# Coarser squares, sums and roots, and pairwise adds in the last five loads, in a power-average pooling kernel (p = 2)

## The chip, the cores and the metric

The kernel runs on one core of one Trainium2 chip. The metric is the device time of one execution in microseconds (us), as the median of several.

## The reference

```python
x = np.random.randn(32, 256, 4096).astype(np.float32)      # p = 2.0, kernel_size = 4
for i in range(out_length):                                # 1024 windows of 4 neighbours
    window = np.abs(x[:, :, 4*i:4*i+4]) ** p
    result[:, :, i] = np.mean(window, axis=-1) ** (1.0 / p)
```

So each output is the root of a quarter of the sum of four squares. 134.2 MB are read and 33.6 MB written.

## The kernel before

The input is taken as 128 rows of columns. 22 loads (18 of 13,184 columns, then three of 6,592 and one of 5,056) go through three input slots (on-chip buffers that are used in turn). Two loads (at the end three, then one) make a group, which has one store. Each load is cut in pieces. A piece is squared in place on ScalarE, summed by fours on VectorE with a reduce, and rooted on ScalarE one piece later.

```python
W, O_W = 13184, 6592
X_SLOTS, O_SLOTS = 3, 2
slots = [[(W, [4416, 4384, 4384])]] * 18          # one slot: (columns of a load, its pieces)
slots += [[(6592, [3296, 3296])] * 2, [(6592, [3296, 3296]), (5056, [2528, 2528])]]
groups = [2] * 9 + [3, 1]                         # loads in each store
late = {7, 8, 9, 10}                              # stores issued from the load queue, after all loads
in_x = {9, 10}                                    # groups whose outputs go into an input slot
# ... (load(), store() and the list of loads cut) ...
def root(g, o, ends):
    nc.scalar.activation(out=o, in_=o, func=Act.Sqrt, scale=1.0 / k)
    if ends and g not in late:
        store(g, nc.scalar)
# ... main loop, over loads i: loads up to two slots ahead are issued first (cut)
    for step in chunks:
        v = xs[i][:, c:c + step]
        nc.scalar.activation(out=v, in_=v, func=Act.Square)
        o = ots[g][:, at + c // k:at + (c + step) // k]
        nc.vector.tensor_reduce(out=o, in_=v.rearrange("p (n j) -> p n j", j=k),
                                axis=mybir.AxisListType.X, op=mybir.AluOpType.add)
        if pending is not None:
            root(*pending)
        c += step
        pending = (g, o, i == firsts[g] + groups[g] - 1 and c == w)
root(*pending)
for g in sorted(late):
    store(g, nc.sync)
```

Of the kernel before, what the change touches and what calls it, by code (L numbers as in the profile page):

```python
# [1 line left out]

# [4 lines left out]


@with_exitstack
def kernel(  # L10
    ctx: ExitStack,
    tc: tile.TileContext,
    x: bass.AP,
    p: float,
    kernel_size: int,
    out: bass.AP,
):






    nc = tc.nc

    assert float(p) == 2.0, "kernel specialized for p == 2"
    k = int(kernel_size)
    assert k == 4, "kernel specialized for kernel_size == 4"

    P = nc.NUM_PARTITIONS  # L30
    fp32 = mybir.dt.float32
    Act = mybir.ActivationFunctionType
    xf = x.rearrange("b c l -> (b c l)")
    of = out.rearrange("b c l -> (b c l)")
    total = xf.shape[0] // P

    W, O_W = 13184, 6592
    X_SLOTS, O_SLOTS = 3, 2
    slots = [[(W, [4416, 4384, 4384])]] * 18
    slots += [[(6592, [3296, 3296])] * 2, [(6592, [3296, 3296]), (5056, [2528, 2528])]]  # L40
    groups = [2] * 9 + [3, 1]
    late = {7, 8, 9, 10}
    in_x = {9, 10}


    loads = [(s, sum(w for w, _ in slot[:j]), *slot[j]) for s, slot in enumerate(slots)
             for j in range(len(slot))]
    n = len(loads)
    assert sum(w for _, _, w, _ in loads) == total

    firsts = [sum(groups[:g]) for g in range(len(groups))]
    assert sum(groups) == n
    group_of = [g for g, count in enumerate(groups) for _ in range(count)]
    columns = [sum(w for _, _, w, _ in loads[firsts[g]:firsts[g] + groups[g]])
               for g in range(len(groups))]

    x_pool = ctx.enter_context(tc.tile_pool(name="x_pool", bufs=X_SLOTS))
    o_pool = ctx.enter_context(tc.tile_pool(name="o_pool", bufs=O_SLOTS))
    ctx.enter_context(tc.manual_schedule())

    def block(flat, g, div):
        at, width = sum(columns[:g]) * P // div, columns[g] * P // div
        return flat[at:at + width].rearrange("(p w) -> p w", p=P)

    slot_tiles = {}
    xs = {}

    def load(i):
        s, at, w, _ = loads[i]
        if at == 0:  # L70
            slot_tiles[s] = x_pool.tile([P, W], fp32, name="xt")
        v = slot_tiles[s][:, at:at + w]
        g = group_of[i]
        src = sum(loads[j][2] for j in range(firsts[g], i))
        nc.sync.dma_start(out=v, in_=block(xf, g, 1)[:, src:src + w])  # L75
        xs[i] = v

    ots = {}

    def store(g, queue):  # L80
        queue.dma_start(out=block(of, g, k), in_=ots[g])  # L81

    def root(g, o, ends):
        nc.scalar.activation(out=o, in_=o, func=Act.Sqrt, scale=1.0 / k)  # L84
        if ends and g not in late:
            store(g, nc.scalar)

    ahead = 0
    while ahead < n and loads[ahead][0] < X_SLOTS - 1:
        load(ahead)  # L90
        ahead += 1
    pending = None
    for i in range(n):
        s, _, w, chunks = loads[i]
        while ahead < n and loads[ahead][0] < s + X_SLOTS:
            load(ahead)
            ahead += 1
        g = group_of[i]
        if i == firsts[g]:
            pool, width = (o_pool, O_W) if g not in in_x else (x_pool, W)  # L100
            t = pool.tile([P, width], fp32, name="ot" if g not in in_x else "xt")
            ots[g] = t[:, 0:columns[g] // k]
        at = sum(loads[j][2] for j in range(firsts[g], i)) // k
        assert sum(chunks) == w
        c = 0
        for step in chunks:
            v = xs[i][:, c:c + step]
            nc.scalar.activation(out=v, in_=v, func=Act.Square)  # L108
            o = ots[g][:, at + c // k:at + (c + step) // k]
            nc.vector.tensor_reduce(  # L110
                out=o, in_=v.rearrange("p (n j) -> p n j", j=k),
                axis=mybir.AxisListType.X, op=mybir.AluOpType.add,
            )
            if pending is not None:
                root(*pending)
            c += step
            pending = (g, o, i == firsts[g] + groups[g] - 1 and c == w)
    root(*pending)
    for g in sorted(late):
        store(g, nc.sync)  # L120


# [1 line left out]
_INS = ['x', 'p', 'kernel_size']  # L124
_OUTS = [((32, 256, 1024), 'float32')]

_NUMBERS = {'p': 2.0, 'kernel_size': 4}


# [26 lines left out]
```

## Time and profile before

| | before |
|---|---|
| time, median (3 runs) | 394.79 us (394.69 to 394.88) |
| span of the profile | 393.0 us |
| DMA packet time, both queues | 99.3% of the span |
| VectorE, ScalarE busy | 72%, 74% |

From the page of before, its busy times (engine, us, share, instructions) and its DMA share in 40 slices (tenths):

```profile
DVE 282.4 (72%) x62; ACT 292.4 (74%) x126; POOL 0.2 (0%) x4
...
DMA  8999999999999999999999999999999999999997
...
q1 hardware_dynamic: 3744, 144.15, 85.3%
q10 hardware_dynamic: 1008, 23.63, 14.0%
```

The last two lines are the load queue (with the late stores) and the store queue: packets, MB, share of the time of 16 DMA engines. Together they fill the span. Neither compute engine does. So the kernel is held by the DMA.

The groups of before by shape give the price of each instruction (count, then busy us in total and mean ns of one, then idle time before it):

```profile
L110 DVE TENSOR_REDUCE ot<-xt 128x1096 f32<-128x4384 f32 x36 | 169.9, 4719 | 6.7 <-ACT xt L108 6.4
L108 ACT ACTIVATE xt<-xt 128x4384 f32<-128x4384 f32 x36 | 138.3, 3843 | 2.9 <-ACT ot L84 2.9
L84 ACT ACTIVATE ot<-ot 128x1096 f32<-128x1096 f32 x36 | 39.7, 1103 | 1.1 <-DVE ot L110 0.9
```

With the other shapes this is 1.04 ns a column for the reduce and 0.84 ns for square and root, plus 0.15 to 0.18 us an instruction.

The timeline of before near the end (start us, us, engine, line, operation):

```profile
380.48 0.89 ACT L84 ACTIVATE xt<-xt 128x824 f32<-128x824 f32 x1 [0.67 <-DVE xt L110]
381.27 2.29 ACT L108 ACTIVATE xt<-xt 128x2528 f32<-128x2528 f32 x1
381.39 6.11 SPq L81 DMA_DIRECT2D out_dram<-xt  x2
...
386.42 0.73 ACT L84 ACTIVATE xt<-xt 128x632 f32<-128x632 f32 x1 [2.23 <-DVE xt L110]
```

The 0.89 us root finishes group 9, and its store is issued at 381.4. The last root ends at 387.15, and the last store follows. The DMA in stretches of that time (stretch, us, VectorE busy, ScalarE busy, POOL, clock, DMA share, GB/s) shows that it never waited for these stores:

```profile
380.00:385.00 5.00, 4.54 (x3) 3.71 (x3) 0.00 (x0) 1.00 0.95 407
385.00:390.00 5.00, 1.38 (x1) 0.73 (x1) 0.00 (x0) 1.00 0.96 411
390.00:393.00 3.00, 0.00 (x0) 0.00 (x0) 0.00 (x0) 1.00 0.35 143
```

From the page, the issue of the last two stores (size, us from issue to landing):

```profile
out_dram<-xt SPq DMA_DIRECT2D x1, 2472.0 KB, 9.3
out_dram<-xt SPq DMA_DIRECT2D x1, 632.0 KB, 5.0
```

### The profile page before, as it was taken

The page shows a single profiled execution, that of the slowest core. Times are in us where ns is not written, and L with a number is a line of the kernel's source. Part 1 is how long each engine was busy: PE and PEld are TensorE (multiplying, and loading weights), DVE is VectorE, ACT ScalarE, POOL GpSimd, SP SyncE. Part 2 cuts the span into 40 slices and gives each one's busy share as a digit, 9 for nine tenths or more (in the row PEclk, how much of TensorE's full clock was granted, in tenths as well). Part 3 has the DMA queues.
Part 4 walks back from the last instruction along what each step waited for, and adds up shares of the span by engine and source line. Part 5 has one row for each costly group of instructions (what it writes and reads, how often), then busy time and mean ns, then how long its engine had stood idle before and what let it go on. Part 6 is the DMA issues. An engine that isn't in the chain of part 4 may idle for free.

```text
span 393.0 us, 316 instructions
## 1 busy us (share of the span) xinstructions
DVE 282.4 (72%) x62; ACT 292.4 (74%) x126; POOL 0.2 (0%) x4
## 2 busy tenths in 40 slices
DVE  0068989494959495949594959595859686899992
ACT  1099986777786768686958695959595949899991
POOL 0000000000000000000000000000000000000000
DMA  8999999999999999999999999999999999999997
GB/s 344 429 429 440 429 424 381 443 459 429 413 440 435 429 427 432 429 440 441 437 448 421 432 462 435 392 429 472 429 413 451 425 429 429 424 429 427 438 429 329
DMA packets 4754, 167.79 MB, mean 427 GB/s; under 512 B 528, under 2 KB 528, under 8 KB 656
## 3 DMA queue, kind: packets, MB, share of 16 engines
q1 hardware_dynamic: 3744, 144.15, 85.3%
q10 hardware_dynamic: 1008, 23.63, 14.0%
q14 instruction: 2, 0.02, 0.0%
HBM read 134.22 MB, written 33.55 MB: 427 GB/s over the span
## 4 chain that ended last, share of the span: by engine, by line
DMA 62%; ACT 19%; DVE 14%; issue 2%; ACTq 0%; SPq 0%
DMA xt<-in_x_dram 62%; ACT xt L108 15%; DVE ot L110 11%; DVE xt L110 3%; ACT ot L84 3%; ACT xt L84 1%; ACTq L81 0%; SPq L75 0%; ACTq L108 0%
## 5 line engine op out<-in xcount | busy, mean ns | idle before, releaser
L110 DVE TENSOR_REDUCE ot<-xt 128x1096 f32<-128x4384 f32 (+1 forms) x54 | 255.4, 4731 | 102.7 <-ACT xt L108 102.4
L108 ACT ACTIVATE xt<-xt 128x4384 f32<-128x4384 f32 (+3 forms) x62 | 230.3, 3716 | 89.2 <-DMA xt<-in_x_dram 86.3
L84 ACT ACTIVATE ot<-ot 128x1096 f32<-128x1096 f32 (+1 forms) x54 | 59.8, 1108 | 1.8 <-DVE ot L110 0.9
L110 DVE TENSOR_REDUCE xt<-xt 128x824 f32<-128x3296 f32 (+1 forms) x8 | 27.0, 3384 | 1.3 <-ACT xt L108 1.2
L84 ACT ACTIVATE xt<-xt 128x824 f32<-128x824 f32 (+1 forms) x8 | 6.7, 841 | 3.0 <-DVE xt L110 2.9
L108 ACT ACT_TABLE_LOAD x1 | 1.3, 1283 | 0.7 <-PEq L137 0.7
L84 ACT ACT_TABLE_LOAD x1 | 1.3, 1283 | 0.0
L137 POOL MEMSET const-bfloat16-1.0<- 128x1 bf16 x1 | 0.1, 101 | 0.0
L137 POOL MEMSET const-uint8-127<- 128x1 uint8 x1 | 0.1, 101 | 0.0
L137 POOL MEMSET const-float32-0.0<- 128x1 f32 x1 | 0.1, 98 | 0.2 <-issue 0.2
L137 POOL MEMSET const-float32-1.0<- 128x1 f32 x1 | 0.1, 98 | 0.0
## 6 DMA issues: line engine op xcount, KB each, us to landing
xt<-in_x_dram SPq DMA_DIRECT2D x18, 6592.0 KB, 39.7
out_dram<-ot ACTq DMA_DIRECT2D x7, 3296.0 KB, 26.4
xt<-in_x_dram SPq DMA_DIRECT2D x3, 3296.0 KB, 24.6
out_dram<-ot SPq DMA_DIRECT2D x2, 3296.0 KB, 29.6
xt<-in_x_dram SPq DMA_DIRECT2D x1, 2528.0 KB, 26.4
out_dram<-xt SPq DMA_DIRECT2D x1, 2472.0 KB, 9.3
out_dram<-xt SPq DMA_DIRECT2D x1, 632.0 KB, 5.0
```

The costliest lines, as they stand in the source:

```text
L84: nc.scalar.activation(out=o, in_=o, func=Act.Sqrt, scale=1.0 / k)
L108: nc.scalar.activation(out=v, in_=v, func=Act.Square)
L110: nc.vector.tensor_reduce(out=o, in_=v.rearrange("p (n j) -> p n j", j=k), axis=mybir.AxisListType.X, op=mybir.AluOpType.add,)
L137: nc = _bacc.Bacc("TRN2", target_bir_lowering=False, num_devices=1)
```

## The change

The intent: fewer and larger instructions in the steady part (one square, one sum a load, one root a store), and a cheaper sum at the end. There two pairwise adds take the place of the reduce: they make half and then a quarter as many results as there are columns, 3/4 in all, where the reduce of before took 1.04 ns for every column. Tiles are now allocated once. The transfers stay as they were.

```diff
-    slots = [[(W, [4416, 4384, 4384])]] * 18
-    slots += [[(6592, [3296, 3296])] * 2, [(6592, [3296, 3296]), (5056, [2528, 2528])]]
+    slots = [[(W, [W])]] * 16 + [[(W, [6592, 6592])]] * 2
+    slots += [[(6592, [6592]), (6592, [6592])], [(6592, [6592]), (5056, [2528, 2528])]]
...
-    in_x = {9, 10}
+    in_x = {9: (2, 0), 10: (2, 4944)}
+    FINE, ENDS, LAG = {21}, {19, 20}, 1      # FINE: a root per piece; ENDS: a root per load
+    PAIRS = 17                               # pairwise adds from this load on
...
+    x_tiles = [x_pool.tile([P, W], fp32, name=f"xt{j}") for j in range(X_SLOTS)]
+    o_tiles = [o_pool.tile([P, O_W], fp32, name=f"ot{j}") for j in range(O_SLOTS)]
...
+    def total_sum(o, v, i):
+        if i < PAIRS:
+            nc.vector.tensor_reduce(...)     # as before
+            return
+        h = v.rearrange("p (m t) -> p m t", t=2)
+        nc.vector.tensor_tensor(out=h[:, :, 0], in0=h[:, :, 0], in1=h[:, :, 1], op=add)
+        q = v.rearrange("p (n j) -> p n j", j=k)
+        nc.vector.tensor_tensor(out=o, in0=q[:, :, 0], in1=q[:, :, 2], op=add)
...
-            if pending is not None:
-                root(*pending)
+            total_sum(ots[g][:, summed:summed + step // k], v, i)
+            while pending and pending[0][0] <= done - LAG:
+                root(*pending.pop(0)[1:])
+            done += 1
...
-            pending = (g, o, i == firsts[g] + groups[g] - 1 and c == w)
+            ends = summed == columns[g] // k
+            if ends or i in FINE or (i in ENDS and c == w):
+                pending.append((done - 1, g, ots[g][:, rooted:summed], ends))
+                rooted = summed
```

More of the change, by code (lines that the diff above doesn't have):

```diff
@@ L55 @@
                for g in range(len(groups))]
-    x_pool = ctx.enter_context(tc.tile_pool(name="x_pool", bufs=X_SLOTS))
-    o_pool = ctx.enter_context(tc.tile_pool(name="o_pool", bufs=O_SLOTS))
+    x_pool = ctx.enter_context(tc.tile_pool(name="x_pool", bufs=1))
+    o_pool = ctx.enter_context(tc.tile_pool(name="o_pool", bufs=1))
+    x_tiles = [x_pool.tile([P, W], fp32, name=f"xt{j}") for j in range(X_SLOTS)]
+    o_tiles = [o_pool.tile([P, O_W], fp32, name=f"ot{j}") for j in range(O_SLOTS)]
     ctx.enter_context(tc.manual_schedule())
@@ L63, in block @@
         return flat[at:at + width].rearrange("(p w) -> p w", p=P)
-    slot_tiles = {}
     xs = {}
@@ L69, in load @@
         s, at, w, _ = loads[i]
-        if at == 0:
-            slot_tiles[s] = x_pool.tile([P, W], fp32, name="xt")
-        v = slot_tiles[s][:, at:at + w]
+        v = x_tiles[s % X_SLOTS][:, at:at + w]
         g = group_of[i]
@@ L86, in root @@
             store(g, nc.scalar)
+    def total_sum(o, v, i):
+        add = mybir.AluOpType.add
+        if i < PAIRS:
+            nc.vector.tensor_reduce(
+                out=o, in_=v.rearrange("p (n j) -> p n j", j=k),
+                axis=mybir.AxisListType.X, op=add,
+            )
+            return
[3 more added lines that the diff above has]
+        nc.vector.tensor_tensor(out=o, in0=q[:, :, 0], in1=q[:, :, 2], op=add)
     ahead = 0
@@ L91 @@
         ahead += 1
-    pending = None
+    pending = []
+    done = 0
     for i in range(n):
@@ L99 @@
         if i == firsts[g]:
-            pool, width = (o_pool, O_W) if g not in in_x else (x_pool, W)
-            t = pool.tile([P, width], fp32, name="ot" if g not in in_x else "xt")
-            ots[g] = t[:, 0:columns[g] // k]
-        at = sum(loads[j][2] for j in range(firsts[g], i)) // k
+            t, first = (o_tiles[g % O_SLOTS], 0) if g not in in_x else (x_tiles[in_x[g][0]], in_x[g][1])
+            ots[g] = t[:, first:first + columns[g] // k]
+            summed = rooted = 0
         assert sum(chunks) == w
@@ L108 @@
             nc.scalar.activation(out=v, in_=v, func=Act.Square)
-            o = ots[g][:, at + c // k:at + (c + step) // k]
-            nc.vector.tensor_reduce(
-                out=o, in_=v.rearrange("p (n j) -> p n j", j=k),
-                axis=mybir.AxisListType.X, op=mybir.AluOpType.add,
-            )
-            if pending is not None:
-                root(*pending)
-            c += step
-            pending = (g, o, i == firsts[g] + groups[g] - 1 and c == w)
-    root(*pending)
+            total_sum(ots[g][:, summed:summed + step // k], v, i)
+            while pending and pending[0][0] <= done - LAG:
+                root(*pending.pop(0)[1:])
+            done += 1
+            c += step
+            summed += step // k
+            ends = summed == columns[g] // k
+            if ends or i in FINE or (i in ENDS and c == w):
+                pending.append((done - 1, g, ots[g][:, rooted:summed], ends))
+                rooted = summed
+    for job in pending:
+        root(*job[1:])
     for g in sorted(late):
```

## The prediction

> **What bounds the kernel now.** The DMA engines. The page's queue table gives them 85.3% + 14.0% = 99.3% of the 393.0 us span: 390.3 us of packet time, against 282 us (72%) for VectorE and 292 us (74%) for ScalarE. In the trace's packet records the first data packet starts 1.6 us into the span, the last ends near 391.6, with no hole between. At the usual packet times (1.947 us per 52,736 B, 0.978 us per 26,368 B) the traffic needs 387.7 us; 2.1 us are slower packets, at the start and at 40 to 70 us. So some 2 us are left to win, whatever the compute does.
>
> Compute touches the end. From the landing of load 17 (339.7 us) the timeline and the windows show ScalarE and VectorE both 90 to 100% busy until the last root (387.1): each small piece goes square, sum, root in turn. Two held-back stores (groups 7, 8) fill the DMA meanwhile. Group 9's store is issued at 381.4, while the queue is still busy, the last one (632 KB) at 387.2; it lands 5.0 us later.
>
> **What the change removes, adds, moves.** The DMA transfers keep count, sizes and layout. From the groups by shape, square and root cost 0.176 us + 0.836 ns a column, the reduce 0.153 us + 1.041 ns a column.
> - One 13,184-column square takes 11.2 us, its sum 13.9, a 6,592-column root 5.7. Some 65 small instructions go, at 0.15 to 0.18 us each: about 10 us of engine time, off the critical path.
> - A slot comes free 25 us after its load lands instead of about 18. Two later loads queue behind it (31 us of transfer at least), so the queue stays fed. Stores go out some 12 us later, which saves no traffic. Worth: 0.
> - Tail. My estimate, stepping both programs through these durations and a 434 GB/s queue, ends them together if a pairwise add runs at one column per 1.04 ns (10.6 us for a 13,184-column load instead of 13.9). With coarse pieces and reduce kept, the tail would be 5 us longer; the adds pay that back.
>
> **The disputed size** is the strided add: operands step two elements in the first add, four in the second. [...] No strided operand is in before's trace. [...] I think full rate likeliest (55%), a slow second add next (30%), both slow 15%.
>
> **Prediction.** 395.4 us, 8 in 10 between 394.0 and 400.5. Faster by over 2%: 1%; within 2%: 87%; slower by over 2%: 12%.
>
> **What would show each step.**
> - DMA share near 99%, packet time near 390 us: the bound holds. No hole between loads 2 and 3 (about 51 us): the feed holds.
> - 16 reduces near 13.9 us, squares near 11.2.
> - First add (6,592 outputs) 7.0 us, second (3,296) 3.6: full rate. [...]
> - The last root ends at 386 to 388 us.
>
> **What would make it wrong.** Slow strided adds [...]; coarse slots letting the DMA run dry early; a store held up by an output tile still being read; packets that become faster under fewer, longer instructions (up to 2 us won).

The forecast came to 395.4 us, 0.6 above before, with 394.0 to 400.5 as its range. Terms of it are cut where marked: two statements on the rate of strided operands, and the sizes given to slow adds (in ns a column and in us, and the time by which a slowed second add was to be known), since no trace of before shows them. "Full rate" is the 1.04 ns a column of before's reduce, carried over to an add that before does not have. The 434 GB/s agrees with the usual packet times: 16 times 52,736 B in 1.947 us is 433 GB/s.

## The result, and the profile after

| | before | after |
|---|---|---|
| time, median (6 runs each) | 394.80 us | 398.08 us (397.87 to 398.33) |
| ratio to before, 95% interval | | 1.0082 (1.0069 to 1.0095) |
| VectorE, ScalarE busy | 282.4, 292.4 us | 275.0, 281.7 us |
| last root ends | 387.15 us | 392.30 us |
| last DMA data packet ends | 391.7 us | 395.0 us |

The change costs 3.3 us, 0.8%, clearly outside the noise and within 2%.

The page of after:

```profile
DVE 275.0 (69%) x32; ACT 281.7 (71%) x40; POOL 0.2 (0%) x4
...
DMA  8999999999999999999999999999999999999967
...
q1 hardware_dynamic: 3744, 144.15, 84.5%
q10 hardware_dynamic: 1008, 23.63, 13.8%
```

Both compute engines do less work. The DMA moves the same packets in 98.3% of a longer span, 389.5 us against 390.3. What is new is the 6 in the last but one slice. The groups of after by shape:

```profile
L93 DVE TENSOR_REDUCE ot<-xt 128x3296 f32<-128x13184 f32 x16 | 222.2, 13886 | 105.1 <-ACT xt L123 105.1
L86 ACT ACTIVATE ot<-ot 128x6592 f32<-128x6592 f32 x9 | 51.2, 5683 | 2.9 <-DVE ot L101 2.9
L99 DVE TENSOR_TENSOR xt<-xt 128x3296 f32<-128x3296 f32 x5 | 17.9, 3587 | 4.6 <-ACT xt L123 4.6
L101 DVE TENSOR_TENSOR xt<-xt 128x1648 f32<-128x1648 f32 x3 | 9.5, 3155 | 0.1
L101 DVE TENSOR_TENSOR ot<-xt 128x1648 f32<-128x1648 f32 x2 | 6.2, 3119 | 0.1
```

Read the last three together. The first add (steps of two elements) makes 3,296 results in 3.59 us, 1.04 ns each after the fixed 0.15 us. The second (steps of four) makes half as many in nearly the same time, 3.155 us: 1.82 ns each. A piece of 6,592 columns costs 6.7 us this way, where the reduce costs 7.02.

The timeline of after, in the tail:

```profile
357.06 3.07 DVE L101 TENSOR_TENSOR ot<-xt 128x1648 f32<-128x1648 f32 x1
...
360.16 5.70 ACT L86 ACTIVATE ot<-ot 128x6592 f32<-128x6592 f32 x1 [2.91 <-DVE ot L101]
...
365.77 11.27 ACT L123 ACTIVATE xt<-xt 128x6592 f32<-128x6592 f32 x2
371.48 3.59 DVE L99 TENSOR_TENSOR xt<-xt 128x3296 f32<-128x3296 f32 x1 [4.62 <-ACT xt L123]
...
384.95 1.58 ACT L86 ACTIVATE xt<-xt 128x1648 f32<-128x1648 f32 x1 [1.45 <-DVE xt L101]
386.43 2.29 ACT L123 ACTIVATE xt<-xt 128x2528 f32<-128x2528 f32 x1
386.55 6.11 SPq L83 DMA_DIRECT2D out_dram<-xt  x2
...
391.57 0.73 ACT L86 ACTIVATE xt<-xt 128x632 f32<-128x632 f32 x1 [2.23 <-DVE xt L101]
```

ScalarE waits 2.91 us for the slow second add. Then it spends 5.70 us in one lumped root, and only then makes the next square. VectorE waits 4.62 us for that. Group 9's root ends 5.2 us later than in before, its store is issued at 386.55, and meanwhile the queue runs dry:

```profile
380.00:385.00 5.00, 4.97 (x3) 3.55 (x3) 0.00 (x0) 1.00 0.58 248
385.00:390.00 5.00, 3.86 (x3) 4.35 (x3) 0.00 (x0) 1.00 0.60 253
390.00:393.00 3.00, 1.50 (x2) 0.73 (x1) 0.00 (x0) 1.00 0.99 422
```

From the page of after, the last store's landing:

```profile
out_dram<-xt SPq DMA_DIRECT2D x1, 632.0 KB, 3.1
```

So the last root is 5.15 us later, the end only 3.3: the last store now lands 3.1 us after its issue instead of 5.0. The emptier queue is the likely reason; it was not tested by itself.

### The profile page after: what moved, and what is told of

Its sections match the earlier page's. It is cut to its first block, busy times and chain, and to the rows that moved or that the text cites. A ratio compares the mean times of both kernels' runs of the same rounds, so it can differ in the third digit from the quotient of the medians.

```text
span 396.2 us, 192 instructions
## 1 busy us (share of the span) xinstructions
DVE 275.0 (69%) x32; ACT 281.7 (71%) x40; POOL 0.2 (0%) x4
## 4 chain that ended last, share of the span: by engine, by line
DMA 47%; ACT 24%; DVE 22%; issue 6%; SPq 0%; ACTq 0%
DMA xt<-in_x_dram 47%; ACT xt L123 18%; DVE ot L93 14%; ACT ot L86 6%; DVE xt L99 4%; DVE xt L101 2%; DVE ot L101 2%; ACT xt L86 1%; ACT L86 0%; SPq L77 0%; ACTq L83 0%
## 5 line engine op out<-in xcount | busy, mean ns | idle before, releaser
L93 DVE TENSOR_REDUCE ot<-xt 128x3296 f32<-128x13184 f32 (+1 forms) x18 | 236.2, 13123 | 110.6 <-ACT xt L123 108.9
L123 ACT ACTIVATE xt<-xt 128x13184 f32<-128x13184 f32 (+2 forms) x25 | 223.1, 8937 | 102.0 <-DMA xt<-in_x_dram 100.2
L86 ACT ACTIVATE ot<-ot 128x6592 f32<-128x6592 f32 x9 | 51.2, 5683 | 2.9 <-DVE ot L101 2.9
L99 DVE TENSOR_TENSOR xt<-xt 128x3296 f32<-128x3296 f32 (+1 forms) x7 | 20.9, 2986 | 5.7 <-ACT xt L123 5.7
L101 DVE TENSOR_TENSOR xt<-xt 128x1648 f32<-128x1648 f32 (+1 forms) x5 | 12.1, 2411 | 0.2
L86 ACT ACTIVATE xt<-xt 128x632 f32<-128x632 f32 (+2 forms) x4 | 6.0, 1492 | 5.0 <-DVE xt L101 5.0
L101 DVE TENSOR_TENSOR ot<-xt 128x1648 f32<-128x1648 f32 x2 | 6.2, 3119 | 0.1
```

Source lines behind the costliest of these rows:

```text
L99: nc.vector.tensor_tensor(out=h[:, :, 0], in0=h[:, :, 0], in1=h[:, :, 1], op=add)
L101: nc.vector.tensor_tensor(out=o, in0=q[:, :, 0], in1=q[:, :, 2], op=add)
```

## The experiments

The theory after this reading: the second add's four-element step makes the loss, through the last root and the hole in the DMA. Rivals: (1) the lumped roots and large pieces in the tail make it; (2) the coarse part ahead of the tail (loads 0 to 15, "the front") or the fixed tiles do. All edits are against after, except where said. Twelve kernels ran: eleven correct, one (strides) wrong and run once.

| run | front, loads 0 to 15 | sums at the end | time, us | its before | ratio (95%) |
|---|---|---|---|---|---|
| compact | coarse | compact adds | 395.88 | 394.67 | 1.0030 (1.0017 to 1.0042) |
| reduce_tail | coarse | reduce | 398.97 | 394.67 | 1.0106 (1.0090 to 1.0121) |
| fine_roots | coarse | slow adds, root per piece | 396.03 | 394.67 | 1.0037 (1.0024 to 1.0049) |
| old_tail | coarse | as in before | 396.26 | 394.67 | 1.0041 (1.0029 to 1.0054) |
| old_front | as in before | slow adds | 396.86 | 394.74 | 1.0052 (1.0039 to 1.0065) |
| old_front_compact | as in before | compact adds | 394.85 | 394.74 | 0.9999 (0.9986 to 1.0011) |
| before_compact | before itself | compact adds | 395.16 | 394.74 | 1.0004 (0.9990 to 1.0018) |
| front_lump | fine, lumped root | compact adds | 394.61 | 394.64 | 0.9999 (0.9985 to 1.0012) |
| front_rootper | coarse, root per load | compact adds | 396.44 | 394.64 | 1.0040 (1.0026 to 1.0053) |
| compact_all | coarse | compact adds in all loads | 395.39 | 394.64 | 1.0017 (1.0004 to 1.0029) |
| front_late | fine, late lumped root | compact adds | 395.53 | 394.96 | 1.0013 (0.9999 to 1.0026) |

### compact: the same two adds without the four-element step

```diff
-        nc.vector.tensor_tensor(out=h[:, :, 0], in0=h[:, :, 0], in1=h[:, :, 1], op=add)
-        q = v.rearrange("p (n j) -> p n j", j=k)
-        nc.vector.tensor_tensor(out=o, in0=q[:, :, 0], in1=q[:, :, 2], op=add)
+        half = v[:, 0:v.shape[1] // 2]
+        nc.vector.tensor_tensor(out=half, in0=h[:, :, 0], in1=h[:, :, 1], op=add)
+        q = half.rearrange("p (n j) -> p n j", j=2)
+        nc.vector.tensor_tensor(out=o, in0=q[:, :, 0], in1=q[:, :, 1], op=add)
```

Expected: 

> Edit: the first pairwise add writes its results next to each other (front half of the same piece), so the second add steps two elements instead of four; all else as after. Theory (the second add's four-element step costs 1.82 ns a column instead of 1.04, 7.4 us more VectorE time in the last five loads, and this delays the last root): second add on 1,648 outputs 1.9 us instead of 3.16, last root ends near 387, no hole in the DMA at 380 to 390 us, time 394.6 to 395.3. Rival 1 (coarse roots and squares in the tail cost the time, not the adds): at least 397. Rival 2 (the coarse front and the fixed tiles cost it): 398.

Measured: 395.88 us (395.57 to 396.14). From the timeline of compact, one second add, the issue of the last two stores, and the last root:

```profile
378.58 1.87 DVE L102 TENSOR_TENSOR xt<-xt 128x1648 f32<-128x1648 f32 x1
...
382.09 5.65 SPq L83 DMA_DIRECT2D out_dram<-xt  x2
...
386.66 0.73 ACT L86 ACTIVATE xt<-xt 128x632 f32<-128x632 f32 x1 [1.77 <-DVE xt L102]
```

One stretch of its DMA, and from its page the last store's landing:

```profile
380.00:385.00 5.00, 3.36 (x4) 4.51 (x4) 0.00 (x0) 1.00 0.98 418
...
out_dram<-xt SPq DMA_DIRECT2D x1, 632.0 KB, 5.9
```

The second add fell from 3.155 to 1.87 us, the last root ends at 387.39 instead of 392.30, and the hole is gone. The loss against before falls from 3.3 to 1.2 us. Taking the four-element step away is thus enough to get back 2.1 us, but the time missed the expectation by 0.6 us: something else costs 1.2 us.

### reduce_tail: no pairwise adds

```diff
-    PAIRS = 17
+    PAIRS = 99
```

Expected: 

> Edit: reduce in all loads, no pairwise adds; all else as after. Theory: the pairwise add of a 6,592-column piece takes 6.75 us even with the slow second add, the reduce 7.02, so this is a little slower than after: 398.5 to 399.5. Rival (the pairwise adds as such are the mistake, the rest of the change is free): 394.8 to 395.3.

Measured: 398.97 us (398.37 to 399.27), 4.3 us over before and about 1 us over after. Even slow, the pairwise adds are no mistake against the reduce; they gain little of what they could.

### fine_roots: a root per piece in the tail, slow adds kept

```diff
-    FINE, ENDS, LAG = {21}, {19, 20}, 1
+    FINE, ENDS, LAG = set(range(16, 22)), {19, 20}, 1
```

Expected: 

> Edit: a root for every piece of loads 16 to 21 instead of one lumped root of 6,592 columns; slow adds kept; all else as after. Theory of the slow add alone: 397.5 to 398.3, as after. Rival 1 (the lumped root holds up the next squares by 5.7 us and starves VectorE, 4.6 us idle at 371 us): 395 or less. If both count, in between: my stepping of the instruction durations says 2.3 us less than after, 395.8.

Measured: 396.03 us (395.71 to 396.88), 1.4 us over before: 1.9 us better than after, with the slow adds untouched. From its timeline, one of the short roots, a second add that is as slow as ever, and the last root:

```profile
368.19 1.57 ACT L86 ACTIVATE xt<-xt 128x1648 f32<-128x1648 f32 x1
...
371.94 3.20 DVE L101 TENSOR_TENSOR xt<-xt 128x1648 f32<-128x1648 f32 x1
...
388.74 0.73 ACT L86 ACTIVATE xt<-xt 128x632 f32<-128x632 f32 x1 [2.24 <-DVE xt L101]
```

The last root ends at 389.47 instead of 392.30. So neither the slow add alone nor the lumped root alone is the cause: the expectation for both together, 395.8, is the one that came near. The chain at the end goes square, sum, root, next square, so a shorter root helps it as a shorter add does. Compact and fine_roots each get back about 2 of the 3.3 us. Whether the two repairs together, behind the coarse front, would gain more than either was not run.

### old_tail: the new front with before's tail

```diff
-    slots = [[(W, [W])]] * 16 + [[(W, [6592, 6592])]] * 2
-    slots += [[(6592, [6592]), (6592, [6592])], [(6592, [6592]), (5056, [2528, 2528])]]
+    slots = [[(W, [W])]] * 16 + [[(W, [4416, 4384, 4384])]] * 2
+    slots += [[(6592, [3296, 3296])] * 2, [(6592, [3296, 3296]), (5056, [2528, 2528])]]
-    FINE, ENDS, LAG = {21}, {19, 20}, 1
-    PAIRS = 17
+    FINE, ENDS, LAG = set(range(16, 22)), {19, 20}, 1
+    PAIRS = 99
```

Expected: 

> Edit: loads 0 to 15 as after (one square, one reduce, one root per store), loads 16 to 21 cut, summed and rooted as in before; fixed tiles kept. If the whole loss is made in the tail's own instructions: 394.8, as before. Rival 2 (the coarse front costs too, since load 15's single square, reduce and lumped root end some 4 us later and the tail starts late): 396 to 397.

Measured: 396.26 us (396.14 to 396.59), 1.6 us over before with the same tail instructions. So the front is not free. The last root of old_tail, from its timeline:

```profile
389.47 0.73 ACT L86 ACTIVATE xt<-xt 128x632 f32<-128x632 f32 x1 [2.23 <-DVE xt L93]
```

It ends 3.05 us later than before's, because the tail starts later: load 15's single square and reduce, and the 5.7 us lumped root of its group, stand in the way of load 16 (its second square starts at 333.17, in before at 328.90).

### old_front and old_front_compact: before's front with the new tail

```diff
-    slots = [[(W, [W])]] * 16 + [[(W, [6592, 6592])]] * 2
+    slots = [[(W, [4416, 4384, 4384])]] * 16 + [[(W, [6592, 6592])]] * 2
-    FINE, ENDS, LAG = {21}, {19, 20}, 1
+    FINE, ENDS, LAG = set(range(16)) | {21}, {19, 20}, 1
```

old_front_compact has the edit of compact besides.

Expected of old_front: 

> Edit: loads 0 to 15 as in before, in three pieces each; tail as in after with the slow second add. Theory (slow add and coarse front both count): between before and after, 396.2 to 397.2. Rival, tail alone: 398.1. Rival, front alone: 394.8.

Expected of old_front_compact: 

> Edit: the compact first add as in the run compact, and loads 0 to 15 cut, summed and rooted in three pieces as in before. The run compact ended 1.2 us above before with no common hole in the DMA: its 16 DMA engines ended up to 2.5 us apart, in before 1.0 us. Theory (the coarse front, with its later stores, leaves one DMA engine behind the others): landings 1 us apart, time 394.4 to 394.9. Rival (the new tail or the fixed tiles make the spread): 395.6 to 396.1, as compact.

Measured: old_front 396.86 us (396.61 to 397.21), old_front_compact 394.85 us (394.69 to 394.87). With the earlier runs this fills a table of two by two, as us over the before of the same rounds:

| | slow second add | compact adds |
|---|---|---|
| coarse front | +3.3 (after) | +1.2 (compact) |
| before's front | +2.1 (old_front) | +0.1 (old_front_compact) |

Before's front makes up only part of the loss when the slow adds stay: in old_front the last root still ends late, as its timeline shows.

```profile
390.61 0.73 ACT L86 ACTIVATE xt<-xt 128x632 f32<-128x632 f32 x1 [2.23 <-DVE xt L101]
```

The slow add, with the lumped roots kept, costs 2.0 to 2.1 us in either row and the coarse front 1.1 to 1.2 in either column. That the columns agree is partly chance, since the front works in two ways. With slow adds the last root sets the end, and the coarse front makes it 0.96 us later (392.30 against 391.34). With compact adds the last root is early enough in both, and the DMA engines set the end (below). The fixed tiles are in all four and cost nothing that shows, since old_front_compact is level with before. One number missed: old_front_compact's landings were 1.6 us apart at the end, not 1.

### before_compact: compact adds in the kernel before

```diff
-            nc.vector.tensor_reduce(...)
+            if i < 17:
+                nc.vector.tensor_reduce(...)      # as before
+            else:
+                ...                               # the two adds of the run compact
```

Expected: 

> Edit to the kernel before: in the last five loads the reduce is replaced by two pairwise adds, compact form; all else as before. Theory (before is held by the DMA to its last byte, and the compact adds are faster but off that path): last root 1 to 5 us earlier, time 394.4 to 394.9. Rival (the tail's compute holds before too): 393.5 or less.

Measured: 395.16 us (394.77 to 395.23), level with before within the interval; the median is 0.3 us above the expected range, which was too narrow. The last root ended at 385.05, 2.1 us earlier than in before, and gained nothing. Before is held by the DMA to its last byte.

### strides: the disputed add by itself

One load, then fp32 adds of 1,648 results at different steps, three of each, and squares. The result is wrong (most of the output is never written); the 140.45 us of this run mean nothing.

```python
def s(t, step, off):
    return t[:, 0:N * step].rearrange("p (n j) -> p n j", j=step)[:, :, off]
# L56 contiguous; L58, L60, L62, L66: both sources at step 2, 3, 4, 8; L64: step 4, neighbours;
# L68 one source at step 4; L70, L72 result at step 2, 4; L74 all three at step 4;
# L76 runs of two neighbours, hop of four. L48, L50, L52: squares, source at step 1, 2, 4; L54: result at 4
```

Expected: 

> Wrong result on purpose: one load, then fp32 adds of 1,648 outputs, three of each kind, with different steps of sources and result, and squares with steps. Theory[...]: step 1 and 2 of the sources 1.87 us, step 4 3.16 us, step 8 no faster than step 4, step 3 between; runs of two adjacent elements with a hop of four 1.87 us; a result step of 2 free, of 4 slow. Rival ([...]any step above one is slow[...]): step 2 near 3 us. Third: only two stepped sources together are slow: one source of step 4 at 1.87 us. No expectation for the squares but that step 2 is free.

Measured, from the groups of strides:

```profile
L66 DVE TENSOR_TENSOR dst<-src 128x1648 f32<-128x1648 f32 x3 | 9.3, 3113 | 0.1
...
L68 DVE TENSOR_TENSOR dst<-src 128x1648 f32<-128x1648 f32 x3 | 9.2, 3082 | 0.1
...
L62 DVE TENSOR_TENSOR dst<-src 128x1648 f32<-128x1648 f32 x3 | 9.2, 3062 | 0.1
...
L60 DVE TENSOR_TENSOR dst<-src 128x1648 f32<-128x1648 f32 x3 | 7.0, 2333 | 0.1
...
L56 DVE TENSOR_TENSOR dst<-src 128x1648 f32<-128x1648 f32 x3 | 5.6, 1875 | 48.3 <-ACT dst L54 48.2
L58 DVE TENSOR_TENSOR dst<-src 128x1648 f32<-128x1648 f32 x3 | 5.6, 1874 | 0.1
L76 DVE TENSOR_TENSOR dst<-src 128x1648 f32<-128x1648 f32 x3 | 5.6, 1874 | 0.1
```

Contiguous operands took 1.875 us (L56) and sources at step 2 took 1.874 (L58), so step 2 is free here, and so are runs of two with a hop (1.874, L76) and a result at step 2 (1.876, L70). Step 3 costs 2.33 us, step 4 3.06, step 8 no more than 3.11. One source at step 4 (3.08 us, L68) or the result alone (3.08, L72) is already as slow as both sources, and all three together are little slower (3.15, L74). The third theory is out, and so is the rival that any step is slow. The ordering is the one that the recorded theory gave in advance; the cause that it named is cut from the record, since the runs show the times alone. ScalarE pays too: a square of 1,648 elements took 1.58 us contiguous, 1.69 with its source at step 2 and 3.12 us with its source at step 4.

### What the coarse front costs when the add is fast: front_lump, front_rootper, compact_all, front_late

In compact the last root ends early enough and the 16 DMA engines have no common hole, yet it ends 1.2 us late. The trace records 16 landings for each transfer (528 for the 33 transfers of before), read here as one for each of the page's 16 DMA engines. Worked out from them, for the last store of each kernel that had no hole before it:

| kernel (no common hole in the tail) | front's squares and sums | from the first engine's landing to the last's, us | to the next to last's, us | time over its before, us: median (the profiled run) |
|---|---|---|---|---|
| before | three pieces | 0.96 | 0.82 | 0 (0) |
| before_compact | three pieces | 1.71 | 1.12 | +0.4 (+0.5) |
| old_front_compact | three pieces | 1.58 | 1.54 | +0.1 (+0.1) |
| front_lump | three pieces | 0.64 | 0.28 | 0.0 (0.0) |
| front_late | three pieces, late stores | 2.03 | 1.05 | +0.6 (+0.7) |
| compact | one piece | 2.52 | 1.00 | +1.2 (+1.5) |
| compact_all | one piece | 2.37 | 1.56 | +0.7 (+1.0) |
| front_rootper | one piece | 2.38 | 0.57 | +1.8 (+0.9) |

One engine comes 1.5 us after the next to last in compact and 1.8 us in front_rootper; the store is done only when it is. In compact 15 engines have landed by 391.8 us, in before by 392.1; the last lands at 393.3 and 392.2. So in these two traces a single engine makes the difference.

The link with the coarse front is looser. The same figure can be read in all thirteen traces at the landing of the last load (near 368 us), before the tail makes a hole in any of them. It is 1.65 to 2.52 us in the seven kernels with one-piece fronts, 0.92 to 1.70 in the five with three-piece fronts, and 1.98 in front_late. The ranges touch, and the seven differ although their fronts are nearly the same program. At the first load, before any square, it is already 0.8 to 1.5. So part of it differs from execution to execution, and the coarse front makes it larger on the whole. The edits, each besides that of compact:

```diff
 front_lump:     slots = [[(W, [4416, 4384, 4384])]] * 16 + ...
 front_rootper:  FINE = set(range(16)) | {21}
 compact_all:    PAIRS = 0
 front_late:     as front_lump, and  while pending and pending[0][0] <= done - (3 if i < 16 else LAG):
```

Expected of front_lump: 

> Edit to the run compact: loads 0 to 15 squared and summed in three pieces each as in before, one lumped root per store kept, so slots come free early and stores leave some 5 us later than in before (9.6 us after the next landing instead of about 5, by the measured durations). If the one-piece squares and sums leave one DMA engine behind: 394.8 to 395.0, landings 1 to 1.7 us apart at the end. If the later store does: between, 395.1 to 395.6. If the lumped root as such: 395.9, as compact.

Expected of front_rootper: 

> Edit to the run compact: loads 0 to 15 keep one square and one sum each, but get a root for every load, so a store leaves 2.7 us earlier than in compact (3,296 columns of root behind the next square instead of 6,592). If the one-piece squares and sums (late slots) leave one DMA engine behind: 395.9, landings 2 us or more apart. If the lumped root does: 394.9. If the time of the store: 395.3 to 395.8.

Expected of compact_all: 

> Edit to the run compact: compact pairwise adds in all 22 loads, 10.6 us instead of 13.9 for a full load. Slots come free 3.3 us earlier, stores leave at the same times as in compact. Theory (sums in the steady part are off the critical path): 395.6 to 396.1, as compact, VectorE busy about 55 us less. If late slots cause the one late DMA engine: less than compact, 395.0 to 395.6. Rival (VectorE time counts throughout): 390 or less.

Expected of front_late: 

> Edit to the run front_lump: the lumped root, and with it the store, waits for the third square of the next load instead of the first, so each store of the front leaves 16.9 us after a landing, as in compact, while squares and sums stay in three pieces and slots come free early. If the late stores leave one DMA engine behind: 395.5 to 396.4, one engine landing 2 us or more after the first. If the one-piece squares and sums (late slots) do: 394.5 to 395.0, landings within 1.7 us.

Measured: front_lump 394.61 us (394.49 to 394.89), so the lumped root by itself is free in the front. front_rootper 396.44 us (395.50 to 396.96), so a root per load cures nothing; it scatters more than the others, and its profiled run is its fastest. front_late 395.53 us (395.17 to 395.68), 0.6 us up and with a late engine of 2.0 us, although squares and sums stay in three pieces: late stores bring part of it, though its interval just reaches no difference. compact_all 395.39 us (394.96 to 395.89), with slots that come free 3.3 us earlier, lies between front_lump and compact, in the range given for late slots as a cause; but its interval overlaps that of compact, so this gain of half a microsecond is not settled. Its page:

```profile
DVE 212.6 (54%) x50; ACT 281.7 (72%) x40; POOL 0.2 (0%) x4
```

VectorE works 62 us less than in after, and against compact, which does the same in the tail, the time falls by only half a microsecond. Sums in the steady part are off the critical path.

What makes one engine late stays open. In after, where the packet records can be chained engine by engine (264 packets each), one engine starts 0.9 us after the first and its packets then take some 2.8 us more than the usual times, against 1.4 to 1.9 us for most; 1.1 of that comes near 72 us, just after the first store is issued at 68.9. Late stores and late slots both seem to count, but each landing figure is of one profiled run, and no experiment here took the slow packets away alone.

## Why the prediction was right or wrong

- The time, 398.08 us, lies within the stated 394.0 to 400.5 and within 2% of before. The point, 395.4, was 2.7 us low. The range held because it left room for the second of the three cases below; the case that the prediction thought likeliest did not happen.
- "What bounds the kernel now" held. The packet time was 390.3 us before and 389.5 after, and neither faster sums in before (before_compact) nor 62 us less of VectorE (compact_all) brought a kernel below the floor.
- The costs of square, sum and root held: the 13,184-column reduce took 13.89 us and the square 11.19, against 13.9 and 11.2 predicted.
- "I think full rate likeliest (55%), a slow second add next (30%)": the second happened. Before's trace has no strided operand. The first add ran at full rate (1.04 ns a result), the second at 1.82 ns. It showed as the last two stores issued at 386.6 and 392.3 us, a hole at 380 to 390, and a last root at 392.3 instead of 386 to 388.
- The size that the prediction gave to a slow second add alone was about twice what it cost, 2.0 to 2.1 us. The last root did move by 4.9 us (392.30 against 387.39), but only part of that reaches the end. In compact the DMA sets the end (last packet near 392.8) and not the root: its last store lands 5.9 us after its issue, in after 3.1. So 2.8 of the 4.9 us fall into slack, and 2.1 are left, as measured.
- "A slot comes free 25 us after its load lands [...]. Worth: 0" failed. The DMA was indeed fed, and no hole came in the front. Yet the front costs 1.1 to 1.2 us: with a slow tail by starting the tail later (old_tail's last root 3.05 us later with before's own tail), with a fast one by one DMA engine that ends late (why it does is open). Asking only whether a queue runs dry missed both. Luck helped here: its size for the slow add was about 2 us too much, 0 for the front 1.2 too little, and the two errors partly cancel.
- "With coarse pieces and reduce kept, the tail would be 5 us longer": 4.3 us (reduce_tail). "The adds pay that back": only about 1 us of it as they were written; at full rate and behind before's front they pay it all (old_front_compact, 0.1 us over before).

So the 3.3 us are about 2.1 for the four-element step together with the lumped roots, of which the repair of either gets back about 2, and about 1.2 for the coarse front. The repaired version, front_lump, is level with before and not faster. No version here beats before: with 390 us of DMA packet time in a span of 393, less arithmetic has almost nothing to win.

## What to carry to other kernels

In a kernel that the DMA fills (99.3% of the span in before), look at what runs after the last load lands: here a chain of square, sum and root set when the last stores were issued, and coarse instructions lengthened it even where they saved busy time (last root at 392.30 us in after, with lumped roots, and at 389.47 in fine_roots). When a reduction is split into pairwise adds, write the half sums next to each other, so that the next add steps two fp32 elements and not four; that edit alone took the add of 1,648 results from 3.16 to 1.87 us. And a queue that never runs dry is not yet a transfer on time: in compact 15 of the 16 engines had landed the last store by 391.8 us, and it was done at 393.3, with the slowest.
